# S5 of a two-layer hybrid trunk in steps of 4 tokens instead of 8, with its products in halves and quarters of the array

## The chip, the cores and the metric

The kernel runs on one core of a Trainium2 chip. Its time is the device time of one execution in microseconds (us); of several runs the median counts. A profile is one more execution, recorded by the hardware.

## The reference

Two residual layers, each with one input projection `h @ w_in` of the normed x (512 tokens, width 2048), four branches that share its columns (MLA attention, S5, RWKV-7, differential attention), a gate, and an output projection. The change touches S5 and the token shift of RWKV:

```python
for l in range(DEPTH):                                    # 2
    h = rms_norm(x, norm_g[l])
    proj = h @ w_in[l]
    c_q, c_kv, k_rope, u_s5, z_rwkv, q_d, k_d, v_d, gate = jnp.split(proj, points, axis=-1)
    ...
    x = x + (mixed @ w_out[l]).astype(x.dtype)

def s5_branch(u, ...):                                    # 32 groups of 16 channels, 64 complex states each
    bu = einsum('bsgc,gpc->bsgp', ug, bb)
    h  = associative_scan over s of h[s] = ab * h[s-1] + bu[s]
    y  = einsum('bsgp,gcp->bsgc', h_re, c_re) - einsum('bsgp,gcp->bsgc', h_im, c_im)
    ...                                                   # + d * u, gelu, gated linear unit

def rwkv7_branch(z, mu, ...):
    z = z + (z_prev - z) * mu                             # the lerp: z_prev is z one token before
```

## The kernel before

Matrices are held transposed, 128 channels on the partitions by 512 tokens. The projections make up most of the program: a column of 128 outputs is 16 steps of 128 inputs, and each step three products of 128x512, since float32 weights and inputs are split into a high and a low part (`XH`, `XL`, `wh`, `wl`). ScalarE casts `wh` (line 243), VectorE subtracts for `wl` (line 244); `big` keeps a ring of three such pieces. The products of a column add up in an accumulator `acc` (two in PSUM) or in one of the six banks `pb`, which everything else uses too.

The order of TensorE's work is written out as the program is built. A class `Clock` holds the planned time of TensorE, and the branches are generators, each of which says with `yield Y[...]` how many microseconds it needs before its next products can be ready; between them the columns of the projections are emitted. The orders of the other engines come from a scheduler with priorities: `tc.high_priority(offset=AHEAD)` moves work that frees an accumulator or prepares weights ahead, and `late` ties an instruction behind the latest weight piece.

In the input projection the columns are the low-rank one (`lo`), then r, k, v of the first and of the second pair of heads, then four of `u`, and so on. They are multiplied without the norm of x, and up to six of them wait (`pend`: two `acc`, four `pb`) until the norm's row `rx` is there. Then `evacuate` is called for each. For `lo` and r, k, v it calls `z_tile`: VectorE multiplies by the norm into `zr` (line 535), ScalarE makes `zd` = `zr` times (1 - mu) (line 537), and VectorE adds `zr` one token back times mu (line 538). `zr` and `zd` have one buffer each.

S5 takes 8 tokens as one step of its state, so that each group has 64 steps. `s5_tables` (line 367 on) makes, in layer 0 beside the first columns and in layer 1 during the output projection of layer 0, the powers of the transition (`pw`) and, in four blocks of 128x512, cosine and sine of each step's angle (`tq`, `tr`, `cs`, lines 469 to 479). Each of 8 units of a layer (`s5_unit`, 4 groups, two units at a time) has these products: transposes of AB into IN; K, from which DMAs lay out the triangular T; IN times U (inputs to states); and, after a rotation by the table, a scan over the steps and a rotation back into `H` (lines 913 to 930), T times U plus CA times H (line 126), which is the unit's output. GpSimd does the products with the sine, ScalarE the copies that swap real and imaginary halves (`sw`).

Of the kernel before, what the change touches and what calls it, by code (L numbers as in the profile page):

```python
# [64 lines left out]
for _n, _w in (("norm_g", 16), ("mu", 13), ("w0", 4), ("a0", 4), ("k_k", 4), ("k_a", 4),  # L65
# [8 lines left out]
PW = {"pr": (0, 9), "pi": (9, 18), "rr": (18, 26), "ri": (26, 34), "m8": (34, 35)}  # L74
NPW = 35
# [12 lines left out]
def consts():  # L88
# [13 lines left out]
    put("qidx", np.broadcast_to(np.arange(64), (128, 64)))  # L102
# [85 lines left out]
def trunk(ctx, tc, io, KT=16, depth=DEPTH):  # L188
# [41 lines left out]
    s5tab = dram("s5tab", [depth, 4, 128, 2, 512])  # L230
# [133 lines left out]
    def s5_tables(pl, l, pace):  # L364
# [34 lines left out]
        for n in (1, 2, 4):  # L399
# [7 lines left out]
        for i in range(8):  # L407
            A.copy(out=pw[:, :, PW["rr"][0] + i], in_=pr[:, :, 7 - i])
            A.activation(out=pw[:, :, PW["ri"][0] + i], in_=pi[:, :, 7 - i], func=AF.Copy, scale=C("sg"))
        m8 = pw[:, :, PW["m8"][0]]  # L410
        V.tensor_tensor(out=m8, in0=mag, in1=mag, op=ALU.mult)
        V.tensor_tensor(out=m8, in0=m8, in1=m8, op=ALU.mult)
        V.tensor_tensor(out=m8, in0=m8, in1=m8, op=ALU.mult)
# [21 lines left out]
        V.tensor_scalar(out=thi, in0=th, scalar1=8.0 / TWO_PI, scalar2=None, op0=ALU.mult)  # L435
# [6 lines left out]
        for q in range(4):  # L442
            g0 = 8 * q
            yield pace
# [32 lines left out]
            cs2 = pl.tile([128, 2, 8, 64], F32, name="cs2", tag="cs2", bufs=2)  # L477
# [52 lines left out]
    def z_tile(ps, mu, m1, rxr, out):  # L530
# [298 lines left out]

    def phases(d):  # L830

        return d.rearrange("(i c) (g q) -> (c g) i q", i=8, g=8)

    def s5_load(sp, l, e, uD):

# [7 lines left out]
        tab = sp.tile([128, 2, 4, 64], F32, name="tab", tag="tab", bufs=3)  # L843
# [531 lines left out]
    class Layer:  # L1375
# [185 lines left out]
        def in_proj(self, begun):  # L1561
            l, pend = self.l, []
            for i, (n, t) in enumerate(ORDER):
# [274 lines left out]
```

## Time and profile before

| | us |
|---|---|
| median of 3 runs | 1981.13 (1977.79 to 1984.48) |
| the profiled execution, its own time | 1977.86 |
| its span, first to last instruction | 1976.0 |
| TensorE busy | 1926.1 (97%) |
| VectorE busy | 1314.7 (67%) |
| ScalarE busy | 870.7 (44%) |
| GpSimd busy | 167.0 (8%) |

The granted clock of TensorE is 0.991 of full speed over the span; 1 is its level of 2.4 GHz, 0.5 that of 1.2 GHz. In the profile PE is TensorE's products, PEld its weight loads, DVE is VectorE, ACT ScalarE, POOL GpSimd. Products overlap one another, so what one costs is read from its start to the next start, not from its length. L126 is the line of the helper that records every product.

### The profile page before, as it was taken

What the parts mean: (1) busy time and instruction counts of PE and PEld (TensorE: products, weight loads), DVE (VectorE), ACT (ScalarE), POOL (GpSimd) and SP (SyncE); (2) the same over time, 40 slices, a digit from 0 to 9 for tenths busy, and PEclk for the clock granted to TensorE, in tenths of its full rate; (3) what the DMA queues carried; (4) which work ended last, traced back from release to release, by engine and by line L of the source; (5) the groups of instructions that cost most, each with busy time, mean ns of one, the idle gap of its engine ahead of it and who ended that gap; (6) DMA issues with size and microseconds to landing.
All of it is one profiled execution on the core that took longest, in us unless ns stands there. A gap on an engine that the chain in (4) does not pass through costs nothing.

```text
span 1976.0 us, 31426 instructions
## 1 busy us (share of the span) xinstructions
PE 1926.1 (97%) x10975; PEld 1565.9 (79%) x10975; DVE 1314.7 (67%) x2883; ACT 870.7 (44%) x1855; POOL 167.0 (8%) x222
## 2 busy tenths in 40 slices
PE   9979999999999999999999999999999999999997
PEld 7867887777778778888888788778788778788787
DVE  6887876556686578747855686674675667766453
ACT  6544335434235446534533334454332544554351
POOL 1101110022000010002001011101010000000001
PEclk9989999999999999999999999999999999999999
DMA  6453546455473437555743454365457326654553
GB/s 213 140 178 117 150 131 163 147 167 174 147 216 103 153 120 238 180 161 188 244 144 123 117 141 140 99 198 176 156 168 225 118 95 211 206 163 156 162 166 117
DMA packets 244734, 316.85 MB, mean 160 GB/s; under 512 B 83680, under 2 KB 109792, under 8 KB 244576
## 3 DMA queue, kind: packets, MB, share of 16 engines
q1 hardware_dynamic: 243200, 313.44, 51.4%
q8 instruction: 86, 1.41, 0.3%
q10 hardware_dynamic: 1376, 1.41, 0.2%
q14 instruction: 72, 0.59, 0.1%
HBM read 238.64 MB, written 73.76 MB: 158 GB/s over the span
## 4 chain that ended last, share of the span: by engine, by line
PE 48%; DMA 2%; DVE 1%; ACT 1%; issue 0%; POOL 0%; SPq 0%; DVEq 0%; ACTq 0%
PE acc L126 39%; PE pb L126 8%; PE pb L130 1%; DMA raw<-in_w_out_dram 1%; DMA yD<-do 0%; DMA xo<-xP 0%; DMA raw<-knD 0%; POOL smag L377 0%; DMA R<-qkD 0%; DVE wl L244 0%; DVE Fo L1647 0%; DMA zr<-yD 0%; ACT wh L243 0%; DMA y<-yD 0%; DVE xo L1613 0%
## 5 line engine op out<-in xcount | busy, mean ns | idle before, releaser
L126 PE MATMUL acc<-XH,wl 128*128 128x512 f32 x1600 | 653.3, 408 | 17.0 <-DVE zr L535 10.7
L126 PE MATMUL acc<-XL,wh 128*128 128x512 f32 x1600 | 627.5, 392 | 1.1 <-DVE XL L494 1.1
L126 PE MATMUL acc<-XH,wh 128*128 128x512 f32 x1600 | 628.1, 393 | 0.0
L243 ACT CAST wh<-raw 128x512 fp32r<-128x512 f32 x559 | 341.8, 617 | 549.0 <-PE acc L126 400.8
L244 DVE TENSOR_TENSOR wl<-raw,wh 128x512 fp32r<-128x512 f32 x559 | 385.8, 694 | 245.5 <-ACT wh L243 241.2
L126 PEld LDWEIGHTS acc<-XH,wl 128*128 128x128 f32 x1600 | 302.1, 189 | 91.8 <-DVE zr L535 11.2
L126 PEld LDWEIGHTS acc<-XH,wh 128*128 128x128 f32 x1600 | 301.7, 189 | 66.0
L126 PEld LDWEIGHTS acc<-XL,wh 128*128 128x128 f32 x1600 | 302.5, 189 | 58.3 <-DVE XL L494 2.7
L126 PE MATMUL acc<-MH,wl 128*128 128x512 f32 x448 | 177.8, 397 | 3.4 <-DVE xo L1613 2.6
L126 PE MATMUL acc<-MH,wh 128*128 128x512 f32 x448 | 174.9, 391 | 0.0
L126 PE MATMUL acc<-ML,wh 128*128 128x512 f32 x448 | 174.7, 390 | 0.0
L126 PEld LDWEIGHTS acc<-MH,wl 128*128 128x128 f32 x448 | 84.2, 188 | 21.9 <-DVE xo L1613 3.4
L126 PEld LDWEIGHTS acc<-MH,wh 128*128 128x128 f32 x448 | 84.1, 188 | 17.9
L126 PEld LDWEIGHTS acc<-ML,wh 128*128 128x128 f32 x448 | 84.2, 188 | 16.3
L1005 ACT ACTIVATE pt<-pb,nb,fc 128x128 f32<-128x128 f32 (+3 forms) x64 | 39.5, 617 | 30.3 <-DVE nb L1004 30.0
L1338 POOL TENSOR_TENSOR sr<-ss,cc 128x1 f32<-128x1 f32 x32 | 19.7, 615 | 326.7 <-DVE ss L1336 247.2
L689 DVE TENSOR_TENSOR tmp<-X 64x30 f32<-64x30 f32 (+14 forms) x120 | 39.7, 331 | 10.8 <-DMA X<-nD 8.4
L1003 DVE TENSOR_REDUCE mx<-pb 128x1 f32<-128x128 f32 (+3 forms) x96 | 45.9, 478 | 0.5
L801 POOL TENSOR_TENSOR rs<-vr,cc 128x16 f32<-128x16 f32 x4 | 12.1, 3028 | 383.1 <-DVE vr L799 383.1
L778 DVE SCALAR_TENSOR_TENSOR SV<-pb,ec,tmp 64x64 f32<-64x64 f32 x96 | 27.2, 283 | 23.6 <-PE pb L126 20.9
L693 DVE TENSOR_TENSOR X<-X,tmp 64x30 f32<-64x30 f32 (+14 forms) x120 | 39.2, 327 | 2.5
L1002 DVE TENSOR_TENSOR pb<-pb,cc 128x128 f32<-128x128 f32 x96 | 26.4, 295 | 21.5 <-PE pb L126 20.9
(408 smaller groups left out, 2804.3 us busy)
## 6 DMA issues: line engine op xcount, KB each, us to landing
raw<-in_w_in_dram SPq DMA_DIRECT2D x415, 256.0 KB, 3.5
raw<-in_w_out_dram SPq DMA_DIRECT2D x128, 256.0 KB, 3.5
gD<-stg SPq DMA_DIRECT2D x32, 256.0 KB, 3.4
xP<-stg SPq DMA_DIRECT2D x19, 256.0 KB, 2.1
xo<-xP SPq DMA_DIRECT2D x19, 256.0 KB, 3.6
zD<-stg SPq DMA_DIRECT2D x18, 256.0 KB, 3.0
s5tab<-cs SPq DMA_DIRECT2D x8, 512.0 KB, 4.7
tab<-s5tab SPq DMA_DIRECT2D x16, 256.0 KB, 4.5
```

The source lines that it names most:

```text
L126: return self.nc.tensor.matmul(out, lhsT=lhsT, rhs=rhs, **kw)
L130: return self.nc.tensor.transpose(out, in_, identity)
L243: x = A.copy(out=wh[:, :n], in_=raw[:, :n])
L244: y = V.tensor_sub(out=wl[:, :n], in0=raw[:, :n], in1=wh[:, :n])
L689: i = V.tensor_tensor(out=t2, in0=X[:, 0:j, j:j + 1].to_broadcast([64, j, n]), in1=X[:, j:j + 1, j + 1:32].to_broadcast([64, j, n]), op=AL ...
L693: V.tensor_tensor(out=X[:, 0:j, j + 1:32], in0=X[:, 0:j, j + 1:32], in1=t2, op=ALU.add)
L778: V.scalar_tensor_tensor(out=SVs[s][T, c + 1, h], in0=po[h][T, 64:128], scalar=ec[T, h, c:c + 1], in1=T1[T, h], op0=ALU.mult, op1=ALU.add)
L801: G.tensor_tensor(out=rs, in0=vr, in1=C("mhalf", 0, 16), op=ALU.pow)
L1002: V.tensor_tensor(out=ps[:, qb * 128:n], in0=ps[:, qb * 128:n], in1=C("neg"), op=ALU.add)
L1003: V.tensor_reduce(out=mx, in_=ps[:, 0:n], axis=AX.X, op=ALU.max)
L1005: A.activation(out=pt, in_=ps[:, 0:n], func=AF.Exp, scale=fcol[:, qb:qb + 1], bias=nb, accum_out=sm)
L1338: G.tensor_tensor(out=sr, in0=ss, in1=C("mhalf", 0, 1), op=ALU.pow)
```

## The change

S5's step becomes 4 tokens. The power tables shrink (9 and 8 powers to 5 and 4), CA from 576 to 320 and AB from 512 to 256 elements a partition; the steps of a group become 128, so the tables for the angles double (8 blocks of 128x512 per layer instead of 4), and so do v, sw, gs and H. A step's inputs of one group now fill 64 partitions, so two groups share the array: IN times U runs in 64-row halves, T times U in 64x64 quarters, CA times H in 64-column halves, 128 columns each, into two banks. One scan over the four groups becomes four scans, since each now takes its factor as a broadcast. The table is loaded at a unit's start, no longer one unit ahead. The planner's entries s1 and s3 and the pace of the tables change. In `z_tile`, `zd` is made by VectorE for the first nine columns of a layer (seven of them are z tiles).

```diff
-PW = {"pr": (0, 9), "pi": (9, 18), "rr": (18, 26), "ri": (26, 34), "m8": (34, 35)}
-NPW = 35
+PW = {"pr": (0, 5), "pi": (5, 10), "rr": (10, 14), "ri": (14, 18), "m4": (18, 19)}
...
-    "z12": 1.5, "ch": 1.4, "h3": 2.58, "h1": 2.73, "h2": 2.54, "gn": 16.96, "s1": 11.34, "s2": 2.8,
-    "s3": 13.65, "glu": 35.7, "lr": 18.14, "kvr": 6.4, "uv": 2.21, "mr": 27.22, "mh": 9.45, "mu": 5.78,
+    "z12": 1.5, "ch": 1.4, "h3": 2.58, "h1": 2.73, "h2": 2.54, "gn": 16.96, "s1": 10.0, "s2": 2.8,
+    "s3": 15.0, "glu": 35.7, "lr": 18.14, "kvr": 6.4, "uv": 2.21, "mr": 27.22, "mh": 9.45, "mu": 5.78,
...
+        for e in range(8):
+            g0 = 4 * e
             yield pace
-
-            qb = C("qidx").unsqueeze(1).to_broadcast([128, 8, 64])
-            tq = pl.tile([128, 8, 64], F32, name="tq", tag="tq", bufs=2)
-            tr = pl.tile([128, 8, 64], F32, name="tr", tag="tr", bufs=2)
-            hb = thi[:, g0:g0 + 8].unsqueeze(2).to_broadcast([128, 8, 64])
-            lb = tlo[:, g0:g0 + 8].unsqueeze(2).to_broadcast([128, 8, 64])
+            if e % 2 == 0:
+                inputs(e // 2)
+                yield pace
+
+            qb = C("qidx").unsqueeze(1).to_broadcast([128, 4, 128])
...
-            cs2 = pl.tile([128, 2, 8, 64], F32, name="cs2", tag="cs2", bufs=2)
+            cs2 = pl.tile([128, 2, 4, 128], F32, name="cs2", tag="cs2", bufs=2)
             sincos(tq, cs2[:, 1], cs2[:, 0], scale=6.2831850)
...
-    def z_tile(ps, mu, m1, rxr, out):
+    def z_tile(ps, mu, m1, rxr, out, quick):
...
         with tc.high_priority(offset=AHEAD):
             V.tensor_tensor(out=zr[:, 1:], in0=ps, in1=rxr, op=ALU.mult)
             d = zp.tile([128, S], F32, name="zd", tag="zd", bufs=1)
-            A.activation(out=d, in_=zr[:, 1:], func=AF.Copy, scale=m1)
+            if quick:
+                V.tensor_scalar(out=d, in0=zr[:, 1:], scalar1=m1, scalar2=None, op0=ALU.mult)
+            else:
+                A.activation(out=d, in_=zr[:, 1:], func=AF.Copy, scale=m1)
             V.scalar_tensor_tensor(out=out, in0=zr[:, 0:S], scalar=mu, in1=d, op0=ALU.mult, op1=ALU.add)
...
-        tab = sp.tile([128, 2, 4, 64], F32, name="tab", tag="tab", bufs=3)
-        SP.dma_start(out=tab.rearrange("p a g q -> p a (g q)"), in_=s5tab[l, t, :, :, 256 * hf:256 * hf + 256])
...
+        pw, bb, U = loaded.pop(e)
+        tab = sp.tile([128, 2, 4, 128], F32, name="tab", tag="tab", bufs=2)
+        SP.dma_start(out=tab.rearrange("p a g q -> p a (g q)"), in_=s5tab[l, e])
...
-        CA, W = t3("CA", 9), t3("W", 9)
+        CA, W = t3("CA", 5), t3("W", 5)
...
-        late(V.tensor_tensor(out=CA, in0=bj(pr), in1=bc(c1, 9), op=ALU.mult))
-        V.tensor_tensor(out=W, in0=bj(pi), in1=bc(c2, 9), op=ALU.mult)
+        late(V.tensor_tensor(out=CA, in0=bj(pr), in1=bc(c1, 5), op=ALU.mult))
...
         yield Y["s1"]
         ps = pb()
-        for g in range(4):
-            PE.transpose(ps[:, g * 128:(g + 1) * 128], AB[:, g].rearrange("p i c -> p (i c)"), ident)
-        A.copy(out=IN.rearrange("p g x -> p (g x)"), in_=ps)
...
+        for p in range(2):
+            PE.transpose(ps[:, p * 128:p * 128 + 128], AB[:, 2 * p:2 * p + 2].rearrange("p h i c -> p (h i c)"), ident)
+        A.copy(out=IN.rearrange("p a x -> p (a x)"), in_=ps[:, 0:256])
...
         for g in range(4):
-            PE.matmul(ps[32 * g:32 * g + 16, 0:128], lhsT=b1[:, g],
-                      rhs=CA[:, g, 0:8].rearrange("p j c -> p (j c)"), start=True, stop=True)
+            PE.matmul(ps[32 * g:32 * g + 16, 0:64], lhsT=b1[:, g],
+                      rhs=CA[:, g, 0:4].rearrange("p j c -> p (j c)"), start=True, stop=True)
...
-        psI = pb()
-        for g in range(4):
-            PE.matmul(psI[:, 64 * g:64 * g + 64], lhsT=IN[:, g], rhs=U8[:, g], start=True, stop=True)
...
-        A.copy(out=swf[0:64], in_=psI[64:128, 0:256])
-        A.copy(out=swf[64:128], in_=psI[0:64, 0:256])
...
+        psI = pb(), pb()
+        for p in range(2):
+            for h, x in enumerate(HS):
+                PE.matmul(psI[h][:, 128 * p:128 * p + 128], lhsT=IN[x, p], rhs=U[x, p], start=True, stop=True)
+        sw, v = t2("sw"), t2("v")
+        for h in range(2):
+            y = psI[h][:, 0:256].rearrange("p (a q) -> p a q", q=128)
+            for a, b in (HS, HS[::-1]):
+                A.copy(out=half(sw, h)[a], in_=y[b])
+            V.tensor_tensor(out=half(v, h), in0=y, in1=half(tab[:, 0], h), op=ALU.mult)
         G.tensor_tensor(out=sw, in0=sw, in1=tab[:, 1], op=ALU.mult)
         V.tensor_tensor(out=v, in0=v, in1=sw, op=ALU.add)
...
-        gs = t2("gs")
-        V.tensor_tensor_scan(out=gs.rearrange("p g q -> p (g q)"), data0=m8.rearrange("p g q -> p (g q)"),
-                             data1=v.rearrange("p g q -> p (g q)"), initial=0.0, op0=ALU.mult, op1=ALU.add)
+        gs = t2("gs", 1)
+        for g in range(4):
+            V.tensor_tensor_scan(out=gs[:, g], data0=m4[:, g].to_broadcast([128, 128]), data1=v[:, g], initial=0.0,
+                                 op0=ALU.mult, op1=ALU.add)
...
         yield Y["s3"]
-        psY = pb()
-        for g in range(4):
-            PE.matmul(psY[:, 64 * g:64 * g + 64], lhsT=T[:, g], rhs=U8[:, g], start=True, stop=False)
-            PE.matmul(psY[:, 64 * g:64 * g + 64], lhsT=CA[:, g, 1:9].rearrange("p j c -> p (j c)"),
-                      rhs=H[:, g, 0:64], start=False, stop=True)
...
+        psY = pb(), pb()
+        for h, x in enumerate(HS):
+            for p, y in enumerate(HS):
+                PE.matmul(psY[h][y, 0:128], lhsT=T[x, p], rhs=U[x, p], start=True, stop=False)
+        for h in range(2):
+            for p, y in enumerate(HS):
+                g = 2 * p + h
+                PE.matmul(psY[h][y, 0:128], lhsT=CA[:, g, 1:5].rearrange("p j c -> p (j c)"), rhs=H[:, g, 0:128],
+                          start=False, stop=True)
...
     def tables(l):
         with sub("tab", l) as st:
-            yield from s5_tables(st, l, 2.5 if l == 0 else 3.0)
+            yield from s5_tables(st, l, 1.6 if l == 0 else 1.8)
...
                 if l in rx:
                     for x in pend:
-                        self.evacuate(*x)
+                        self.evacuate(*x, i < 9)
```

The program's order on TensorE for the output of the first two units of layer 0 (`acc` is a projection's accumulator, numbers tell buffers apart). Before, the first unit's run, with T and CA in turn four times (the first of the pairs shown):

```order
L126 MATMUL acc_2013<-XH_78,wh_2064 128x512
L126 MATMUL pb_2071<-U8_1596,T_1830 128x64
L126 MATMUL pb_2071<-H_1909,CA_1685 128x64
L126 MATMUL pb_2071<-U8_1596,T_1830 128x64
L126 MATMUL pb_2071<-H_1909,CA_1685 128x64
```

After, the run of both units:

```order
L126 MATMUL acc_2097<-XH_78,wh_2118 128x512
L126 MATMUL pb_2125<-U_1643,T_1863 64x128 x2
L126 MATMUL pb_2126<-U_1643,T_1863 64x128 x2
L126 MATMUL pb_2125<-H_1956,CA_1734 64x128 x2
L126 MATMUL pb_2126<-H_1956,CA_1734 64x128 x2
L126 MATMUL pb_2140<-U_1651,T_1887 64x128 x2
L126 MATMUL pb_2141<-U_1651,T_1887 64x128 x2
L126 MATMUL pb_2140<-H_1986,CA_1755 64x128 x2
L126 MATMUL pb_2141<-H_1986,CA_1755 64x128 x2
L126 MATMUL acc_2097<-XH_78,wl_2119 128x512
```

Each product is now 64x128 in place of 128x64, all of T stand ahead of those of CA, and the second unit stands right behind the first, where before nine products of a column lay between them.

VectorE's order around the sixth and seventh `zr` of layer 0 (`tq`, `tr`, `cs` are S5's tables, `stg` the lerp's output, `tmp` RWKV's). Before:

```order
L476 TENSOR_TENSOR tq<-tq,tr 128x512 x2
L583 SCALAR_TENSOR_TENSOR tmp<-cc,tmp 128x512
L244 TENSOR_TENSOR wl<-raw,wh 128x512
L535 TENSOR_TENSOR zr<-pb,rxr 128x512
L479 TENSOR_SCALAR cs_1017<-cs_1017,cc 128x512
L479 TENSOR_SCALAR cs_1153<-cs_1153,cc 128x512
L335 TENSOR_SCALAR cs_1017<-cs_1017 128x512
L592 TENSOR_SCALAR tmp<-tmp 128x512
L335 TENSOR_SCALAR cs_1153<-cs_1153 128x512
L538 SCALAR_TENSOR_TENSOR stg<-zr,pvt,zd 128x512
L535 TENSOR_TENSOR zr<-acc,rxr 128x512
L538 SCALAR_TENSOR_TENSOR stg<-zr,pvt,zd 128x512
```

After:

```order
L541 TENSOR_TENSOR zr<-pb,rxr 128x512
L476 TENSOR_TENSOR tq<-tq,tr 128x512
L478 TENSOR_TENSOR tr<-cc,stlo 128x512
L544 TENSOR_SCALAR zd<-zr,dv 128x512
L478 TENSOR_TENSOR tr<-cc,stlo 128x512
L479 TENSOR_TENSOR tq<-tq,tr 128x512
L547 SCALAR_TENSOR_TENSOR stg<-zr,pvt,zd 128x512
L479 TENSOR_TENSOR tq<-tq,tr 128x512
L480 TENSOR_SCALAR tr<-tq 128x512
L541 TENSOR_TENSOR zr<-acc,rxr 128x512
L480 TENSOR_SCALAR tr<-tq 128x512
L481 TENSOR_TENSOR tq<-tq,tr 128x512
```

Between these two `zr` stood two more steps of a table block (lines 479 and 335) and RWKV's row; now there stand the lerp's `zd` and six instructions of the next table block.

VectorE's order around the second unit's `H`. Before:

```order
L915 TENSOR_TENSOR v<-v,sw 128x256
L535 TENSOR_TENSOR zr<-acc,rxr 128x512
L883 TENSOR_TENSOR W<-pw,bb 128x4x128
L244 TENSOR_TENSOR wl<-raw,wh 128x512
L920 SCALAR_TENSOR_TENSOR gs<-m_1941,v 128x256
L538 SCALAR_TENSOR_TENSOR stg<-zr,pvt,zd 128x512
L927 TENSOR_TENSOR v<-gs,tab 128x256
L917 COPY m_2347<-pw 128x256
L918 MEMSET m_2347 128x4
L244 TENSOR_TENSOR wl<-raw,wh 128x512
L930 TENSOR_TENSOR H<-v,sw 128x4x64
```

After:

```order
L937 SCALAR_TENSOR_TENSOR gs<-pw,v 128x128 x3
L547 SCALAR_TENSOR_TENSOR stg<-zr,pvt,zd 128x512
L937 SCALAR_TENSOR_TENSOR gs<-pw,v 128x128
L244 TENSOR_TENSOR wl<-raw,wh 128x512
L898 TENSOR_TENSOR AB<-pw,bb 128x256
L944 TENSOR_TENSOR v<-gs,tab 128x512
L893 TENSOR_TENSOR CA<-pw,bb 128x320
L898 TENSOR_TENSOR AB<-pw,bb 128x256
L900 TENSOR_TENSOR AB<-AB,W 128x256
L895 TENSOR_TENSOR CA<-CA,W 128x320
L698 TENSOR_TENSOR tmp<-X 64x30
L947 TENSOR_TENSOR H<-v,sw 128x4x128
```

Between the scan and `H` stood one `wl` and the start of another unit's chain (L917, L918); now the scan is four instructions, and CA and AB of the next units, one `wl` and a row of RWKV (L698) stand there.

## Rows read from the trace of the kernel before

**Rows 1.** Busy time of TensorE: us, share of the span, instructions.

```profile
PE 1926.1 (97%) x10975; PEld 1565.9 (79%) x10975; DVE 1314.7 (67%) x2883; ACT 870.7 (44%) x1855; POOL 167.0 (8%) x222
```

**Rows 2.** TensorE's waits by releaser: us in total, times, longest.

```profile
PE acc L126 <- DVE zr L535: 10.7, 1, 10.7
PE acc L126 <- DVE wl L244: 5.5, 7, 1.8
...
PE pb L126 <- DVE H L930: 2.1, 1, 2.1
```

**Rows 3.** TensorE's timeline: start us, us, operation, stationary tile, xcount.

```profile
186.04 0.60 PE L130 MATMUL pb<-cc,AB 128*128 128x128 f32 x4
186.56 0.41 PE L126 MATMUL pb<-CA,bb 128*16 128x128 f32 x8
186.91 0.66 PE L130 MATMUL pb<-cc,AB 128*128 128x128 f32 x4
...
188.48 1.10 PE L126 MATMUL pb<-U,IN 128*128 128x64 f32 x8
189.39 0.48 PE L126 MATMUL acc<-XH,wl 128*128 128x512 f32 x1
...
203.42 0.33 PE L126 MATMUL pb<-U,T 128*128 128x64 f32 x2
...
205.12 0.48 PE L126 MATMUL acc<-XH,wl 128*128 128x512 f32 x1
```

**Rows 4.** TensorE's timeline at products in parts of the array.

```profile
195.20 1.16 PE L126 MATMUL pb<-Q,SV 64*128 64x128 f32 x16
196.29 0.50 PE L126 MATMUL acc<-XH,wl 128*128 128x512 f32 x1
...
300.55 0.45 PE L126 MATMUL pb<-SV,NM 64*64 64x64 f32 x8
300.93 0.45 PE L126 MATMUL pb<-SV,BKt 128*64 128x64 f32 x8
...
304.39 0.39 PE L126 MATMUL acc<-XL,wh 128*128 128x512 f32 x1
304.61 0.39 PE L126 MATMUL acc<-XH,wh 128*128 128x512 f32 x1
304.93 0.69 PE L126 MATMUL pb<-SV,Q 128*64 128x64 f32 x16
305.55 0.50 PE L126 MATMUL acc<-XH,wl 128*128 128x512 f32 x1
```

**Rows 5.** VectorE's timeline before the seventh `zr`.

```profile
87.24 0.69 DVE L469 TENSOR_TENSOR tq<-cc,sthi 128x512 f32<-128x512 f32 x1
87.84 0.68 DVE L244 TENSOR_TENSOR wl<-raw,wh 128x512 fp32r<-128x512 f32 x1
88.45 0.42 DVE L470 TENSOR_SCALAR tr<-tq 128x512 f32<-128x512 f32 x1
88.78 0.76 DVE L335 TENSOR_SCALAR cs<-cs 128x512 f32<-128x512 f32 x2
...
106.73 0.98 DVE L335 TENSOR_SCALAR cs<-cs 128x512 f32<-128x512 f32 x1 [1.74 <-ACT cs L334]
...
110.06 0.69 DVE L535 TENSOR_TENSOR zr<-acc,rxr 128x512 f32<-128x512 f32 x1
```

**Rows 6.** Windows: us, busy PE, PEld, DVE, ACT, POOL (count), clock, DMA, GB/s.

```profile
72.80:110.10 37.30, 27.28 (x119) 21.43 (x117) 34.40 (x67) 27.52 (x44) 3.15 (x8) 0.92 0.46 153
110.10:209.70 99.60, 95.00 (x514) 76.29 (x514) 78.25 (x133) 39.96 (x74) 11.66 (x22) 0.96 0.51 148
908.30:1001.00 92.70, 91.87 (x405) 75.50 (x404) 79.15 (x183) 48.41 (x91) 0.30 (x5) 1.00 0.67 216
```

**Rows 7.** The window behind TensorE's wait for `zr`, same columns.

```profile
110.81:120.00 9.19, 9.19 (x35) 8.04 (x36) 6.40 (x12) 3.47 (x5) 1.96 (x2) 0.63 0.52 144
```

**Rows 8.** VectorE's timeline, first unit of S5.

```profile
200.39 0.41 DVE L930 TENSOR_TENSOR H<-v,sw 128x256 f32<-128x256 f32 x1
```

More of the change, by code (lines that the diff above doesn't have):

```diff
@@ L55 @@
 for _n, _w in (("ident", 128), ("bones", 128), ("maskS", 128), ("neg", 128), ("reset", 512),
-               ("qidx", 64), ("bo2", 2), ("one", 2), ("invm", 1), ("invd", 1), ("ssin", 1),
+               ("qidx", 128), ("bo2", 2), ("one", 2), ("invm", 1), ("invd", 1), ("ssin", 1),
                ("sg", 1), ("mhalf", 32), ("e", 32)):
@@ L101, in consts @@
     put("reset", np.broadcast_to((np.arange(512) % 64 != 0), (128, 512)))
-    put("qidx", np.broadcast_to(np.arange(64), (128, 64)))
+    put("qidx", np.broadcast_to(np.arange(128), (128, 128)))
     put("bo2", (p[:, None] // 64 == np.arange(2)[None, :]))
@@ L398, in s5_tables @@
         V.tensor_tensor(out=pi[:, :, 1], in0=mag, in1=sn, op=ALU.mult)
-        for n in (1, 2, 4):
+        for n in (1, 2):
             br = pr[:, :, n:n + 1].to_broadcast([128, 32, n])
@@ L406, in s5_tables @@
         V.tensor_scalar(out=pw[:, :, a:b], in0=pr, scalar1=C("sg"), scalar2=-1.0, op0=ALU.mult, op1=ALU.mult)
[L407 to L413, printed above, removed]
+        for i in range(4):
+            A.copy(out=pw[:, :, PW["rr"][0] + i], in_=pr[:, :, 3 - i])
+            A.activation(out=pw[:, :, PW["ri"][0] + i], in_=pi[:, :, 3 - i], func=AF.Copy, scale=C("sg"))
+        m4 = pw[:, :, PW["m4"][0]]
+        V.tensor_tensor(out=m4, in0=mag, in1=mag, op=ALU.mult)
+        V.tensor_tensor(out=m4, in0=m4, in1=m4, op=ALU.mult)
         SP.dma_start(out=s5pw[l], in_=pw)
@@ L441, in s5_tables, with inputs @@
         cs = []
-        for q in range(4):
+        def inputs(q):
             g0 = 8 * q
-            yield pace
             sb = pl.tile([128, 2, 2, 64], F32, name="ssb", tag="ssb", bufs=2)
@@ L482, in s5_tables @@
             yield pace
-            if q:
-                late(SP.dma_start(out=s5tab[l, q - 1], in_=cs[q - 1].rearrange("p a g q -> p a (g q)")))
+            if e:
+                late(SP.dma_start(out=s5tab[l, e - 1], in_=cs[e - 1].rearrange("p a g q -> p a (g q)")))
         yield pace + 4.0
-        late(SP.dma_start(out=s5tab[l, 3], in_=cs[3].rearrange("p a g q -> p a (g q)")))
+        late(SP.dma_start(out=s5tab[l, 7], in_=cs[7].rearrange("p a g q -> p a (g q)")))
     def absorb(sp, k, x, pvt, sqs, first):
@@ L883, in s5_unit @@
-        V.tensor_tensor(out=W[:, :, 0:8], in0=bj(ri), in1=bc(b2, 8), op=ALU.mult)
-        V.tensor_tensor(out=AB, in0=AB, in1=W[:, :, 0:8], op=ALU.add)
-        IN = sp.tile([128, 4, 128], F32, name="IN", tag="IN", bufs=1)
+        AB, W = t3("AB", 4), t3("W", 5)
+        V.tensor_tensor(out=AB, in0=bj(rr), in1=bc(b1, 4), op=ALU.mult)
+        V.tensor_tensor(out=W[:, :, 0:4], in0=bj(ri), in1=bc(b2, 4), op=ALU.mult)
+        V.tensor_tensor(out=AB, in0=AB, in1=W[:, :, 0:4], op=ALU.add)
+        IN = sp.tile([128, 2, 128], F32, name="IN", tag="IN", bufs=2)
@@ L899, in s5_unit @@
-        T = sp.tile([128, 4, 128], F32, name="T", tag="AB", bufs=2)
+            A.copy(out=K[:, g], in_=ps[32 * g:32 * g + 16, 0:64])
+        T = sp.tile([128, 2, 64], F32, name="T", tag="AB", bufs=2)
         G.memset(T, 0.0)
-        for i in range(8):
-            SP.dma_start(out=T[16 * i:16 * i + 16, :, 16 * i:128], in_=K[:, :, 0:128 - 16 * i])
+        for h in range(2):
+            for i in range(4):
+                o = 64 * h + 16 * i
+                SP.dma_start(out=T[o:o + 16, :, 16 * i:64], in_=half(K, h)[:, :, 0:64 - 16 * i])
@@ L951, in load @@
             for x, d in ((u, uD), (y, ysD)):
-                SP.dma_start(out=x.rearrange("p (i q) -> p i q", i=8), in_=phases(d[t]))
+                SP.dma_start(out=x.rearrange("p (i q) -> p i q", i=4), in_=phases(d[t]))
             return u, y
@@ L1378, in __init__ @@
             self.yD = dram(f"yD{l}", [16, 128, S])
-            for n, shape in (("uD", [4, 128, S]), ("ysD", [4, 128, S]), ("qkD", [1024, S]),
+            for n, shape in (("uD", [4, 64, 2 * S]), ("ysD", [4, 64, 2 * S]), ("qkD", [1024, S]),
                              ("vD", [4, 128, S]), ("aD", [7, 128, S]), ("knD", [4, 128, S]),
@@ L1472, in others, with evacuate @@
             self.finish("others")
[L1475 removed]
+        def evacuate(self, n, t, ps, quick):
             l, rxr = self.l, rx[self.l][1]
```

78 lines of the change are left out of this document (40 added, 38 removed).

## The prediction

> **What bounds the kernel now.** I read the table of busy time first. TensorE is busy for 97% of the span [rows 1], so a microsecond that TensorE no longer works is a microsecond off the end, unless a wait takes its place. The list of TensorE's waits by what ended them comes next [rows 2]: one wait of 10.7 us for VectorE's `zr`, seven for `wl` with 5.5 us together, one of 2.1 us for `H`. The change touches the causes of all three. So two questions stand: what S5's products cost TensorE before and after, and whether VectorE, which gets more to do, comes later at those three places.
>
> **S5's products on TensorE.** There are 8 units in each of 2 layers, 16 in all. From start to start in TensorE's timeline [rows 3] one unit costs 0.52 (four transposes, 186.04 to 186.56), 0.35 (K, to 186.91), 0.91 (IN times U, 188.48 to 189.39) and 1.70 (T times U and CA times H in turn, 203.42 to 205.12): 3.48 us, 55.7 us in all. A record of the full-array products thus takes 0.91/8 = 0.114 or 1.70/16 = 0.106 us.
>
> The trace has products in parts of the array, in RWKV [rows 4]. A 64-row half (128 columns moved, the new form of IN times U) takes 1.09/16 = 0.068 us a record, a 64-column half with 64 columns moved 0.62/16 = 0.039, quarters 0.38/8 = 0.048. So parts of the array do run side by side: a record in a half that moves 128 columns takes less than a full-array record that moves 64. After the change I take: two transposes 0.29 (half of 0.52 and a start), K with half the columns 0.25 (between 0.18 and 0.35), IN times U 8 x 0.068 and a start = 0.61, T times U 0.38 (quarters, by the row), CA times H 8 x 0.068 and a start = 0.57. Together 2.10, which saves 1.38 a unit: **-22.1 us**. The ends: all 34 records at 0.039 cost 1.33, which saves 34.4; a price of 0.106 to 0.114 for each record, as for the full array, makes 0.91 + 0.85 + 0.85 + 0.26 + 0.35 = 3.22 and saves only 4.2. I stay near the tiled rows, since they are the same shapes.
>
> A tiled run has an entry and an exit. Before the run at 304.93 the step is 0.32 (from 304.61) where a plain one is 0.22 (from 304.39), and the first product behind it lasts 0.50 where plain ones last 0.39 [rows 4]: 0.10 + 0.11, about 0.2 us. Each unit has one more such run in effect, since the runs of two units stand together: 16 x 0.2 = **+3.2 us** (ends 0 and 9.6, three runs a unit).
>
> The Trainium skill, page "TensorEngine Tiling (Array Packing)", section "Key Properties" of "Tiling Modes", says that a change of tiling mode drains the array, and its page "TensorE: Matmul & The Clock Gate" puts a drain at about 175 ns. By those figures, as an estimate, four changes a unit would cost 16 x 4 x 0.175 = 11.2 us in place of 3.2, and the sum would come out 8 us higher, at -0.6. The rows show 0.1 us at a change, so the measured step decides here.
>
> **VectorE before the seventh `zr`.** Until the norm of x is ready, TensorE runs ahead; six columns then wait to be evacuated, and TensorE stands until 110.8, when the seventh `zr` (start 110.06) has freed its accumulator [rows 2, 5]. In this stretch VectorE is busy 34.40 of 37.30 us [rows 6], so what is put in front of that `zr` delays it. VectorE's prices, start to start [rows 5]: 0.60 for two operands of 128x512 (87.24 to 87.84), 0.33 for one operand (88.45 to 88.78). By the program's order 62 instructions stand from the first to the seventh `zr` before and 80 after, at those prices 32.6 and 39.6 us: 7.0 more, six of them lerp products at 0.33, the rest table work. Against it, the lerp no longer waits for ScalarE, and VectorE's idle time in this stretch is 37.30 - 34.40 = 2.90; I credit 2.7 of it (1.74 alone is before the row at 106.73, and that one is a sine that stays on ScalarE). The `zr` comes 7.0 - 2.7 = **+4.3 us** later (ends: +7.0 with nothing credited, and -10.7 if the stall closes, below). The first `zr` starts as before: the rows ahead of it sum to 47.4 and 46.9 us.
>
> **VectorE up to the second unit of S5.** From the first `zr` to the second unit's `H` the order holds 197 instructions before (104.8 us) and 246 after (124.4): 19.6 us more, of which 7.0 are counted above. The other 12.6 us lie between 110.1 and 209.7, where VectorE is free for 99.60 - 78.25 = 21.35 us [rows 6]. That is cover, but not all in the right place: after the seventh `zr` a block of table rows now stands ahead of the next `wl`, and the second `H` is already 2.1 us late [rows 2]. Ends 0 and 12.6; I take **+3 us**, near the hidden end.
>
> **Tables of layer 1.** The same four more blocks of tables fall on the seam of the layers, 91.2 us of work in place of 75.7: 15.5 more. From 908.3 to 1001.0 VectorE has 92.70 - 79.15 = 13.55 us free [rows 6], so **+2 us** are left over (ends 0, since more room follows, and 15.5).
>
> **S5's chain on the vector engines.** Per unit the halves of `sw` are now four copies, GpSimd's two products double in size and one scan becomes four. I estimate 2.5 to 3.5 us more per unit, while the planner's entry s3 gives 1.35 more. The first unit's `H` ends at 200.80 [rows 8], 2.6 us ahead of the unit's run at 203.42 [rows 3]; so a unit like it has cover for the difference. Where it is gone, at the pair's second unit, the wait grows: **+1 us** (ends 0, and 8 with four such units). U's and ys's longer DMA runs, the shorter power tables and the smaller CA and AB lie beside all this and count as nothing; CA and AB save VectorE some 0.7 us a unit, which is in the counts above for the first pair.
>
> **Sum.** -22.1 + 3.2 + 4.3 + 3 + 2 + 1 = -8.6 us. The profiled execution took 1977.86 us, so 1969.3; the median of the runs, 1981.13, lies 3.3 above it, so about 1972 us for the runs.
>
> **Rivals.**
> *B, the stall closes.* The two waits of the lerp on ScalarE are what kept VectorE from the seventh `zr`, and with them gone the 10.7 us go, with the half-speed stretch behind them: from 110.81 to 120.00 the granted clock is 0.63 [rows 7], so TensorE loses 9.19 x 0.37 = 3.4 us. Then -14.1 stands in place of +4.3: 1954 us. For it speaks that `zr` and `zd` have one buffer each, so that each lerp holds up the next evacuation; against it, that VectorE was 92% busy in this stretch and gets more.
> *C, the other side: VectorE's table work falls on TensorE.* All 19.6 us of layer 0 reach TensorE, as a longer stall at the seventh `zr` and late `wl` and `H` behind it, with a second restart at half speed (3.4): -22.1 + 3.2 + 19.6 + 3.4 + 2 + 1 = +7.1, 1988 us. It decides once layer 0 loses more than 22.1 - 3.2 - 3 = 15.9 us. For it: VectorE is the last to end at all three places. Against it: the 21.35 us free.
> *D, the parts of the array don't run side by side* in these shapes: the saving is 4.2 and the sum +9.3, 1990 us. Against it stand the tiled rows; for it, that T and CA now write one bank in turns from different halves.
> *E, the changes of shape cost more*: at three runs a unit with 0.2 us each, 9.6 in place of 3.2, the sum is -2.2 and the time 1979 us. For it: T times U and CA times H have shapes of their own, so the array changes more often than before. Against it: no row shows more than 0.1 us at one change.
> The Trainium skill's rule on drains, cited above, would end beside E, at about 1981 us.
>
> **Chances.** Forecast 0.48, B 0.20, C 0.18, D 0.04, E 0.05, and 0.05 for something that I don't see. About 0.3% (6 us) is what a measurement of this kernel can tell from no change: under 1975 is faster, over 1987 slower. The forecast's own range is 1963 to 1982, so a third of it is "same"; B is faster; two thirds of C, D and some of the unseen are slower, and E is "same": faster 0.52, same 0.27, slower 0.21. The range of 1950 to 1989 leaves out the better part of B's lower half and of C's and D's upper.
>
> **What would show it.** In the new trace: S5's runs at about 2.1 us a unit, the runs of tiled products with steps like [rows 4] (if IN times U takes 0.9 us or more, D is right); the wait for `zr` in the list, at about 15 us (B: gone or a few us; C: 20 and more); waits for `wl` and `H` of some 5 and 3 us; no TensorE wait near the seam of the layers above 2 us. I am wrong if the waits of [rows 2] change by more than 10 us in sum, or S5's runs by less than 0.8 or more than 1.8 us a unit.

## Result and the profile after

The changed kernel takes 2010.73 us in the median of 4 runs (2005.79 to 2011.19), the kernel before 1980.2. The ratio is 1.0149 (1.0131 to 1.0166): 30 us slower, where 8.6 us faster was forecast and 1989 was the upper end. By the prediction's own sign of being wrong, the waits of [rows 2] for `zr`, `wl` and `H` went from 18.3 to 41.2 us, by more than its 10 us, while S5's runs cost 1.4 us less a unit, inside its limits of 0.8 and 1.8.

The list of TensorE's waits of the changed kernel (us in total, times, longest), which answers to [rows 2], and below it the busy times of the page, which answer to [rows 1]:

```profile
PE acc L126 <- DVE zr L541: 16.4, 1, 16.4
PE pb L126 <- DVE H L947: 15.1, 4, 7.4
PE acc L126 <- DVE wl L244: 9.7, 12, 3.1
PE acc L126 <- ACT XH L498: 6.3, 2, 6.0
```

```profile
PE 1925.8 (96%) x10943; PEld 1550.2 (77%) x10943; DVE 1358.7 (68%) x2988; ACT 881.0 (44%) x1899; POOL 185.4 (9%) x222
```

TensorE is as busy as before (1926.1), although its work became less: a stretch at half clock counts as busy. I add up both timelines of TensorE, from each product's start to the next start (up to the last product), and set apart the waits and, as an estimate, what half clock adds (half of each such stretch, outside waits). S5's products go from 56.4 to 33.9 us, all others from 1859.3 to 1863.8, waits from 38.2 to 71.8, and half clock from 10.2 to 27.9: -22.5 + 4.5 + 33.6 + 17.7 = 33.3, the difference of the spans (2009.3 and 1976.0). So S5's saving is there, and waits with the clock behind them cost 51 us. Up to the last product the kernel before has four stretches at half clock, 27 us long together, the changed kernel nine, 75 us long.

TensorE's timeline of the changed kernel at the first pair of units, which answers to [rows 3] (start us, us, operation, stationary tile, count):

```profile
196.50 0.38 PE L130 MATMUL pb<-cc,AB 128*128 128x128 f32 x2
196.81 0.31 PE L126 MATMUL pb<-CA,bb 128*16 128x64 f32 x8
...
199.80 1.11 PE L126 MATMUL pb<-U,IN 64*128 64x128 f32 x16
200.74 1.59 PE L126 MATMUL pb<-Q,SV 64*128 64x128 f32 x16
...
215.52 0.45 PE L126 MATMUL pb<-U,T 64*64 64x128 f32 x8
215.90 0.66 PE L126 MATMUL pb<-H,CA 128*64 128x128 f32 x8
216.49 0.45 PE L126 MATMUL pb<-U,T 64*64 64x128 f32 x8
224.34 1.12 PE L126 MATMUL pb<-H,CA 128*64 128x128 f32 x8 [7.40 <-DVE H L947]
```

IN times U of both units is one run of 16 records, 0.94 us or 0.059 a record; T times U takes 0.38 (215.52 to 215.90), CA times H 0.59. These are near the prices that the prediction took from [rows 4] (0.068 a record, 0.38 and 0.57). But the second unit's output waits 7.4 us for `H`. What happens in its chain, in the timelines of GpSimd and of VectorE:

```profile
202.69 1.30 POOL L933 TENSOR_TENSOR sw<-sw,tab 128x512 f32<-128x512 f32 x1 [4.93 <-ACT sw L931]
209.55 1.29 POOL L942 TENSOR_TENSOR sw<-sw,tab 128x512 f32<-128x512 f32 x1 [5.56 <-ACT sw L941]
211.09 1.29 POOL L933 TENSOR_TENSOR sw<-sw,tab 128x512 f32<-128x512 f32 x1 [0.25 <-ACT sw L931]
...
219.72 2.71 POOL L942 TENSOR_TENSOR sw<-sw,tab 128x512 f32<-128x512 f32 x1 [1.48 <-ACT sw L941]
```

```profile
223.49 0.20 DVE L698 TENSOR_TENSOR tmp<-X 64x30 f32<-64x30 f32 x1 [2.18 <-DMA X<-nD]
223.61 0.67 DVE L947 TENSOR_TENSOR H<-v,sw 128x512 f32<-128x512 f32 x1
```

GpSimd does the sine products of the first unit at 202.69 and 209.55, and those of the second after them, at 211.09 and 219.72, here in 2.71 us. VectorE then stands for 2.18 us at an RWKV row that waits for a DMA, with `H` behind it; 1.1 us of this lie behind the end of GpSimd's product at 222.43, before which `H` could not start. From its IN times U to its `H` (224.28) the second unit needs 24.5 us; the plan gives it 15.0. Before, its IN times U came 2.9 us after the first's (191.36 and 188.48) and its `H` 18.3 us after that:

```profile
191.36 1.10 PE L126 MATMUL pb<-U,IN 128*128 128x64 f32 x8
209.27 0.41 DVE L930 TENSOR_TENSOR H<-v,sw 128x256 f32<-128x256 f32 x1
```

The seam of the layers, VectorE and then TensorE of the changed kernel:

```profile
1021.25 0.68 DVE L481 TENSOR_TENSOR tq<-tq,tr 128x512 f32<-128x512 f32 x1
1021.85 0.48 DVE L484 TENSOR_SCALAR cs<-cs,cc 128x512 f32<-128x512 f32 x1
1022.24 0.68 DVE L1620 TENSOR_TENSOR xo<-acc,xo 128x512 f32<-128x512 f32 x1
```

```profile
1023.77 0.80 PE L126 MATMUL acc<-XH,wl 128*128 128x512 f32 x1 [5.96 <-ACT XH L498]
```

The tables of layer 1 still run (1021.25, 1021.85) where the last `xo` of the output projection is due, and TensorE waits 5.96 us for the `XH` made from it. Of the 4.40 us that VectorE works from 1017.84 to this `xo`, three table rows take 1.3. Before, the last table row came at 966, 30 us ahead of the seam, and the first product of layer 1 did not wait for the last `xo` at all, but stood ahead of it:

```profile
997.26 0.39 PE L126 MATMUL acc<-XH,wl 128*128 128x512 f32 x1
998.02 0.69 DVE L1596 TENSOR_TENSOR xo<-acc,xo 128x512 f32<-128x512 f32 x1 [0.41 <-issue]
```

This is a matter of order. The output projection's order of columns is built from those that were done ahead (`part` in `out_proj`). With 9 done ahead, as before, column 0 comes first; with 10, as in the changed kernel, it comes last; and the first product of a layer reads the `XH` of column 0.

The windows behind the three longest waits (us, busy times with counts, clock, DMA, GB/s), the first of which answers to [rows 7]:

```profile
116.70:124.00 7.30, 7.27 (x25) 6.46 (x26) 7.30 (x16) 4.39 (x8) 2.27 (x2) 0.50 0.28 99
224.30:232.00 7.70, 7.66 (x31) 6.07 (x32) 6.66 (x22) 1.35 (x4) 0.11 (x1) 0.75 0.50 143
1023.70:1031.00 7.30, 7.22 (x18) 5.34 (x19) 2.80 (x6) 1.68 (x4) 0.14 (x2) 0.55 0.74 242
```

### The profile page after: what moved, and what is told of

Read it like the earlier page. It is cut to its first block, busy times and chain, and to the rows that moved or that the text cites. A ratio compares the mean times of both kernels' runs of the same rounds, so it can differ in the third digit from the quotient of the medians.

```text
span 2009.3 us, 31589 instructions
## 1 busy us (share of the span) xinstructions
PE 1925.8 (96%) x10943; PEld 1550.2 (77%) x10943; DVE 1358.7 (68%) x2988; ACT 881.0 (44%) x1899; POOL 185.4 (9%) x222
## 4 chain that ended last, share of the span: by engine, by line
PE 56%; DVE 7%; DMA 6%; issue 3%; ACT 2%; SPq 1%; POOL 1%; DVEq 0%; ACTq 0%; POOLq 0%
PE acc L126 44%; PE pb L126 11%; PE pb L130 2%; DVE wl L244 1%; DMA xo<-xP 1%; DMA raw<-in_w_out_dram 1%; DMA qs<-qrD 1%; DMA gt<-ysD 0%; ACT wh L243 0%; DVE tmp L698 0%; DMA w2a<-gD 0%; POOL sdt L377 0%; POOL smag L377 0%; DVE X L702 0%; DMA ks<-aD 0%
## 5 line engine op out<-in xcount | busy, mean ns | idle before, releaser
L126 PE MATMUL acc<-XH,wl 128*128 128x512 f32 x1600 | 656.7, 410 | 32.2 <-DVE zr L541 16.4
L698 DVE TENSOR_TENSOR tmp<-X 64x30 f32<-64x30 f32 (+14 forms) x120 | 41.0, 342 | 11.2 <-DMA X<-nD 8.6
L126 PE MATMUL acc<-MH,XL 128*128 128x256 f32 x128 | 36.6, 286 | 1.0 <-DVE xo L1637 1.0
```

Source lines behind the costliest of these rows:

```text
L126: return self.nc.tensor.matmul(out, lhsT=lhsT, rhs=rhs, **kw)
L698: i = V.tensor_tensor(out=t2, in0=X[:, 0:j, j:j + 1].to_broadcast([64, j, n]), in1=X[:, j:j + 1, j + 1:32].to_broadcast([64, j, n]), op=AL ...
```

## Experiments

Numbers in brackets are ratios to the kernel before with their 95% intervals; the changed kernel is at 1.0149. The kernel before was timed beside each group of runs (medians of 1976.5 to 1980.2 us), so differences between runs are taken from the ratios; with these intervals they are good to some 3 to 5 us. A "step" counts TensorE's products of the projections, 6336 in each kernel: the time of the same step in two traces tells how far one is behind.

**Half the tables** (`a_halftab`). Every second block of table arithmetic is left out, ScalarE's sines with it.

```diff
         for e in range(8):
...
+            if e % 2 == 0:
                 V.tensor_tensor(out=tq, in0=qb, in1=hb, op=ALU.mult)
...
```

> The changed kernel with the arithmetic of every second block of S5's angle tables left out (its place is filled with the block before, so the output is not that of S5); all else stays. Theory W, VectorE's doubled table work makes the longer wait for zr and the wait at the seam of the layers: the wait for zr falls from 16.4 to 8 to 11 us, the wait of 6.0 us for XH near 1024 us goes with the half-speed stretch behind it, and the time falls by 18 to 25 us, to 1986 to 1993. Rival R1, the table work is hidden and the loss is all in S5's units: within 4 us of 2010.7.

1995.87 us, 1.0097 (1.0080 to 1.0115): 10 us back, about half of what was expected. The wait for `zr` is again that of before, the waits for `H` stay, and the seam keeps a wait of 4 us, although the last table row now comes at 979, 37 us ahead of the product that waits (1015.99):

```profile
PE pb L126 <- DVE H L949: 15.4, 4, 7.7
PE acc L126 <- DVE zr L543: 10.9, 1, 10.9
...
PE acc L126 <- ACT XH L500: 4.4, 2, 4.0
```

**More time for each unit** (`a_s3`): `"s3": 15.0` becomes 24.0.

> The changed kernel with one number of the planner raised: s3, the time that a unit of S5 is given from its IN times U to its output, 24.0 in place of 15.0. Theory W, two units now start together and share VectorE, ScalarE and GpSimd, so the second is due too early: the waits for H fall from 15.1 to under 3 us, three or four half-speed stretches go with them, and the time falls by 12 to 22 us, to 1989 to 1999. Rival R2, the chain is bound elsewhere (the longer S5 puts the wait at another product, or is given back where MLA begins later): within 5 us of 2010.7.

2006.36 us, 1.0140 (1.0122 to 1.0159): within what R2 said. No wait for `H` is left in the list, and at step 2448, near the end of layer 0's input projection, this kernel is 12.6 us ahead of the one before where the changed kernel is 17.5 behind. From there to step 3312 it loses 30.5 us again: S5 ends 36 us later in the plan, with it the branches, and less of the output projection is left beside which the tables could run.

**The lerp** (`a_lerp_act`, `b_lerp`): `self.evacuate(*x, i < 9)` with `False` for the condition; and the diff's hunk of `z_tile` alone on the kernel before.

> The changed kernel with the lerp product back on ScalarE in all columns. Theory W, the lerp on VectorE costs about 0.33 us a column in the stretch before the seventh zr and saves waits of the same size: the wait for zr stays within 3 us of 16.4, the time within 4 us of 2010.7. Rival R3, the lerp on VectorE is what lengthened the stall: 6 us less wait and about 8 us less time. Rival B of the prediction, in weaker form (the lerp on VectorE helps, and the tables hide it): 5 us or more longer.

> The kernel before with the lerp product of the first nine columns on VectorE, nothing else changed. Theory W: the wait for zr stays within 3 us of 10.7, the time within 4 us of 1980. Rival R3: the wait is 13 us or more and the time 1984 or more. Rival B of the prediction: the wait falls below 4 us, and the time to about 1966 to 1972.

2010.02 us, 1.0159 (1.0146 to 1.0173), and 1979.31 us, 1.0010 (1.0001 to 1.0020). The lerp costs or gives nothing that can be told. It does lengthen the wait for `zr`, from 10.8 to 16.4 with the doubled tables and from 10.7 to 13.0 without them, against theory W's 3 us in the first; but between steps 432 and 576 the kernel without it loses 5.9 us against the one before, the changed kernel 3.2, and by step 1152 they stand 19.0 and 21.8 us behind. So most of the shorter wait is lost again at later ones.

**Tables elsewhere** (`a_mid`, `a_mid_s3`, `a_pool`, `a_pace`): tables of layer 1 in `others` of layer 0 behind GLU, alone and with s3 at 24; every second block's arithmetic on GpSimd; the paces of before.

```diff
-            PE.spawn(tables(l + 1), 1)
...
                 yield from s5_glu(gp, l, P, self.uD, self.ysD, self.yout)
+            if l + 1 < depth:
+                yield from tables(l + 1)
```

```diff
+            X = G if e % 2 else V
...
-            V.tensor_tensor(out=tq, in0=qb, in1=hb, op=ALU.mult)
+            X.tensor_tensor(out=tq, in0=qb, in1=hb, op=ALU.mult)
```

> The changed kernel with the tables of layer 1 made in layer 0, between GLU and MLA, where VectorE is half free, and no longer beside the output projection; all else stays. Theory W, the table work on the seam is what makes TensorE wait there: the wait of 6.0 us for XH near 1024 us and the half-speed stretch behind it go, the ten microseconds lost from step 3168 to step 3312 of the projections fall to 2 or less, and the time falls by 8 to 14 us, to 1997 to 2003. Rival R5, the tables only move: MLA and the differential attention come later by as much, and the time stays within 5 us of 2010.7.

> Both edits at once: tables of layer 1 between GLU and MLA, and s3 at 24.0. With s3 alone the projections of layer 0 ran 13 us ahead of the kernel before and lost 30 us on the seam. Theory W, that loss is the tables, squeezed into an output projection with less left to do: without them the gain stays, and the time is 1960 to 1980, at or below the kernel before. Rival R6, the loss is the later end of the branches themselves: 1995 or more.

> The changed kernel with the multiplications, roundings and differences of every second block of S5's tables on GpSimd in place of VectorE; the same results. Theory W, VectorE's load is the cause at zr and at the seam: the wait for zr falls to 9 to 13 us, the loss on the seam to under 7, and the time to 1993 to 2002, near that with half the blocks left out (1996). Rival R7, GpSimd's products are slow beside a busy VectorE (its products of 128x512 took 1.3 to 3.3 us in the units) and the tables come later than S5 wants them: 2008 or more.

> The changed kernel with the planner's steps between the parts of a table block at 2.5 and 3.0 us as before the change, in place of 1.6 and 1.8. Theory W, it is the sum of VectorE's work that is too much, not its order: the wait for zr falls to 11 to 14 us, but what is saved comes back as waits for wl and H or as a later S5, and the time stays within 6 us of 2010.7, with the seam worse by up to 6 us. Rival R8, the faster pace put the table rows ahead of the evacuations and is the cause: 2002 or less.

2051.19 us, 1.0369 (1.0348 to 1.0389); 2057.52, 1.0407 (1.0388 to 1.0427); 2029.04, 1.0267 (1.0248 to 1.0285); 2008.81, 1.0160 (1.0142 to 1.0177). In `a_mid` the step from 3168 to 3312 costs 1.9 us in place of 10.0, as expected, but this doesn't show the tables' share alone: with 12 columns done ahead in place of 10, column 0 is no longer last. The branches end later, with 25 us lost between steps 2880 and 3024: W's total failed in both runs, and a later branch is a bound of its own. `a_pool` is slower, as R7 said, but not because S5 gets its tables late: the waits for `H` stay at 15.0 us and that for `zr` falls to 10.6, as W said, but those for `wl` rise from 9.7 to 28.7. VectorE's groups of `a_pool` between 937 and 1020 us (count, busy us, mean ns, idle before):

```profile
L244 DVE TENSOR_TENSOR wl<-raw,wh 128x512 fp32r<-128x512 f32 x23 | 23.1, 1002 | 0.8 <-ACT wh L243 0.7
...
L508 DVE TENSOR_TENSOR sqs<-sqs,sq 128x512 f32<-128x512 f32 x10 | 9.6, 964 | 0.0
L1621 DVE TENSOR_TENSOR xo<-acc,xo 128x512 f32<-128x512 f32 x11 | 7.5, 685 | 2.0 <-DMA xo<-xP 1.6 <-PE acc L126 0.3
```

`wl` takes 1002 ns on average where it takes 686 in the changed kernel, `xo`, which reads PSUM, still 685. The paces change nothing in sum (and leave the wait for `zr` at 16.4, where W had 11 to 14).

**The units apart** (`a_stag`, `a_swdve`, `a_stag_sw`, `a_stag_half`): the second unit's first wait in the plan is 8 us longer; both sine products on VectorE; both; and the first with half the tables.

```diff
             loaded[e] = s5_load(sp, l, e, uD)
-            yield Y["ld"]
+            yield Y["ld"] + 8.0 * e
```

```diff
-        G.tensor_tensor(out=sw, in0=sw, in1=tab[:, 1], op=ALU.mult)
+        V.tensor_tensor(out=sw, in0=sw, in1=tab[:, 1], op=ALU.mult)
...
-        G.tensor_tensor(out=sw2, in0=sw2, in1=tab[:, 1], op=ALU.mult)
+        V.tensor_tensor(out=sw2, in0=sw2, in1=tab[:, 1], op=ALU.mult)
```

> The changed kernel with the second unit of S5 of each layer begun 8 us later in the plan, so that two units run in turn and not together; s3 stays at 15.0. Theory W, a pair that starts together is what makes H late: the waits for H fall from 15.1 to under 4 us, three half-speed stretches go, S5 ends 8 us later and not 36 as with s3 at 24, and the time falls by 8 to 16 us, to 1995 to 2003. Rival R6, a later S5 gives back what the waits save: within 5 us of 2010.7.

> The changed kernel with the two products of each unit by the sine table on VectorE in place of GpSimd. Theory W, GpSimd's products of 128x512 (1.3 to 3.3 us, and VectorE slower beside them) make the chain of a unit long: at 0.6 us each the waits for H fall to 8 to 11 us and the time by 4 to 9 us. Rival R9, VectorE is what is short: 32 products more (19 us) make waits for wl and H longer, and the time rises by 3 us or more.

> Both edits at once: the second unit 8 us later and the sine products on VectorE. Theory W: no wait for H above 1 us is left, and the time is 1989 to 1999. Rival R9 with R6: 2008 or more.

> The second unit 8 us later, and the arithmetic of every second table block left out (so the output is not that of S5). Theory W, the two causes are apart and add up: 10 to 14 us for the tables as before and 8 to 16 for the pairs, so 1978 to 1992; what then stands above the kernel before is the seam, where half the tables already left 7 us. Rival R10, they do not add up, because one wait covers for the other: within 4 us of 1996.

1986.09 us, 1.0042 (1.0027 to 1.0057); 2014.67, 1.0187 (1.0171 to 1.0204); 1988.23, 1.0053 (1.0038 to 1.0067); 1971.45, 0.9971 (0.9958 to 0.9984). Eight microseconds in the plan give back 21, more than the 8 to 16 expected. The waits of `a_stag` hold no `H` at all; the first are:

```profile
PE acc L126 <- DVE zr L541: 16.4, 1, 16.4
PE acc L126 <- DVE wl L244: 10.9, 11, 3.1
PE pb L126 <- ACT PT L1039: 6.9, 9, 1.4
PE acc L126 <- ACT XH L498: 3.9, 1, 3.9
```

Half clock costs 14.2 us here in place of 27.9, the waits 56.7 in place of 71.8. The sine products on VectorE make the waits for `H` longer (23.9 us, 6 times), those for `wl` not (9.6); the time rises as R9 said. With the units apart they change nothing that can be told (1.0053 and 1.0042). With half the tables as well another 14 us go: the two causes add up, and 1971 is below the 1978 to 1992 expected.

**Which layer's tables, and whose gain** (`a_stag_half0`, `a_stag_half1`, `a_stag_act`, `b_stag`): half the tables in one layer alone; two instructions of each block on ScalarE; the units apart in the kernel before.

```diff
-            sincos(tq, cs2[:, 1], cs2[:, 0], scale=6.2831850)
-            V.tensor_scalar(out=cs2[:, 1], in0=cs2[:, 1], scalar1=C("sg"), scalar2=-1.0,
-                            op0=ALU.mult, op1=ALU.mult)
+            sincos(tq, cs2[:, 1], cs2[:, 0], scale=-6.2831850, act=True)
+            A.activation(out=cs2[:, 1], in_=cs2[:, 1], func=AF.Copy, scale=C("sg"))
```

> Second unit 8 us later, and every second table block's arithmetic left out in layer 0 alone (so the output is not that of S5). Both layers' blocks left out gave 1971.5 against 1986.1 with all blocks. Theory W, most of these 14.6 us is layer 0's: the wait for zr from 16.4 to 10.9, its half-speed stretch from 20.5 to 13.7 us long, and the wait for wl near 168 us with its stretch; 9 to 11 us, so 1975 to 1977, and the seam stays as it is (the step from 3168 to 3312 at 8 to 9 us). Rival R11, most of it is the seam's: 1981 to 1984.

> Second unit 8 us later, and every second table block's arithmetic left out in layer 1 alone (so the output is not that of S5). Theory W: layer 0 stays at 16.4 us for zr, the seam's step falls from 8.8 to about 4, and the time is 1981 to 1983. Rival R11: 1975 to 1978.

> Second unit 8 us later, and two of the ten instructions of each table block moved from VectorE to ScalarE (the sign of the sine and 1 - 2 s^2 of the cosine); the results are the same. It takes 0.73 us of VectorE's work a block away, 5.8 us a layer, a third of what the four more blocks of a layer cost. Theory W: a third of the 14.6 us comes back, the wait for zr falls to 12 to 15 us, and the time is 1979 to 1984. Rival R12, ScalarE is as full as VectorE in these stretches and casts wh later: 1986 or more.

> The kernel before with the second unit of S5 begun 8 us later, nothing else changed. Theory W, before the change the two units were apart by 2.9 us and their chains shorter, with one wait for H of 2.1 us: the wait and its half-speed stretch of 6.8 us go at most, and the time stays within 6 us of 1977 (the gain of 21 us from the same edit on the changed kernel repairs a loss that the change made). Rival R13, the later second unit is a gain of its own, from another order of the branches: 1965 or less.

1977.17 us, 0.9998 (0.9986 to 1.0009); 1982.33, 1.0022 (1.0010 to 1.0033); 1981.34, 1.0013 (1.0001 to 1.0025); 1971.13, 0.9967 (0.9955 to 0.9980). Against `a_stag` half of layer 0's tables are worth 0.44% (8.7 us), half of layer 1's 0.20% (4 us, hardly clear of the intervals). The seam keeps 4.2 us (steps 3168 to 3312) with half of layer 1's tables. The units apart are a gain of 6.5 us in the kernel before too, so that, if the gains add, about 15 of the 21 us repair what the change lost.

**Two last versions** (`a_stag14_act`, `a_stag_act_pace`): `a_stag_act` with 14.0 in place of 8.0, and with layer 0's pace at 2.5.

> The version with two table instructions on ScalarE, and the second unit 14 us later in place of 8, half of a unit's 27.8 us in the plan, so that the units alternate evenly. Theory W, at 8 us no wait for H is left, so the pairs' cause is gone and more distance only delays S5 by 6 us: within 5 us of 1981. Rival R14, units of even distance load VectorE and the clock more evenly (fewer half-speed stretches in 250 to 310 us): 1968 to 1976, below the kernel before.

> The same version with the second unit 8 us later and the pace of layer 0's tables at 2.5 us as before the change, layer 1's left at 1.8. With both old paces the projections were 7 us less behind at the end of layer 0 than with the new ones, and lost this on the seam. Theory W, VectorE's load at the start of layer 0 is the larger part of the tables' cost, so spreading it gives 3 to 8 us: 1973 to 1978. Rival R8 reversed, S5 begins 20 us later and the branches end later: 1984 or more.

1982.51 us, 1.0018 (1.0007 to 1.0029), and 1984.16, 1.0026 (1.0017 to 1.0035): the distance of 8 us was enough, and the slower pace gives nothing (the time is at R8's bound). No complete version of the change gets below the kernel before; the kernel before with its units apart does.

## Why the prediction was wrong

- **S5's products**: right. -22.1 was forecast, -22.5 came. The other products grew by 4.5 us against 3.2 for the entries and exits; but they grew by about 4 us in `b_stag` too, whose products are those of before, so the entries have no clean price here. The Trainium skill's drains ("TensorEngine Tiling (Array Packing)", "Key Properties"), 11.2 us as estimated, are more than all of that (the estimate took about 175 ns from "TensorE: Matmul & The Clock Gate", section "Single matmul latency", and left out the page's further term for the columns moved); the measured sum decides.
- **S5's chain, "+1 us (ends 0, and 8)"**: this step failed. The waits for `H` went from 2.1 to 15.1 us, and with the clock behind them the pairs cost about 15 us (21 with what the kernel before would gain too), beyond the upper end of 8. I compared the longer chain of one unit with the cover of the first unit, 2.6 us. The order showed that both units' runs now stand together, and I took from it only the price of an entry. The second chain runs behind the first on engines that both share, so its time was the one to compare with s3: 24.5 us against 15.0.
- **Half clock**: the sum has no term for it. The longest waits (`zr`, `XH`, the four for `H`, one for `wl`) each had a stretch at half clock behind them, many short ones had none; together the stretches cost 17.7 us more than before. Only rivals B and C had such a price, 3.4 us.
- **VectorE in layer 0, +4.3 and +3**: the size was near. The wait for `zr` grew by 5.7 us, and half the tables give back 8.7 in all. But the 2.7 us credited to the lerp did not come: the lerp on VectorE lengthens this wait, by 2.3 us in `b_lerp` and by 5.6 against `a_lerp_act`.
- **The seam, +2**: too small. Steps 3168 to 3312 lost 10.0 us (8.8 in `a_stag`, of which half the tables of layer 1 give back 4.6). I read 13.55 us of free time in [rows 6] as one stock. But the tables began later against the seam (GpSimd's first table row at 916.40 us after, 894.00 before, with the projections 17 us later), and one more column had been done ahead (20 `xP` in the page, 19 before), so that less of the output projection lay beside them. That column also put column 0 last in the order, which no term of the prediction has: in `a_halftab`, with as many table rows as before and none of them near the seam, the same steps still lose 6.9 us. How the 10.0 us divide between order and tables no run shows by itself.
- **Rivals**: B is refuted by the lerp's runs. C gave the right side with another price: VectorE's tables alone cost 13 to 14 us and would not have turned 18 us of saving. D is refuted by the tiled rows, E by the other products' growth of 4.5 us in all against its 9.6.

Together: -18.0 us on TensorE's products, about +15 for the pairs and +13 to 14 for the tables make some +10; the other 20 stay open. They show when both causes are undone: `a_stag_half` (0.9971) is no faster than `b_stag` (0.9967), although its products cost TensorE 18 us less; its waits are 43.7 against 34.1 us and its half clock 12.3 against 4.1. Split at step 3312, one column behind the seam, almost all of this lies in layer 0: waits of 32.1 against 24.4 us and half clock of 12.2 against 3.9, in four stretches that `b_stag` doesn't have (at 252, 279, 490 and 999 us). Behind the seam the waits are 11.2 against 9.5, half clock is the same, and of the 9.9 us that S5's products save there 7.3 reach the end. The waits in layer 0 are spread over many small groups (`wl`, RWKV, MLA, the seam), and no run took them away. That the cheaper S5 brings each branch's work to VectorE closer together would fit, but wasn't tried.

## What to carry to other kernels

When a step of a planned pipeline becomes cheaper, look at what now stands next to what: two chains that start together share every engine behind them, and the due time is that of the second one. Price a new wait of the bounding engine together with the half-clock stretch that may stand behind it. And free time of a helper engine counts only where it lies ahead of the due time, not as a sum over a window. Where a program builds an order from counts, look at what a count of one more puts last.

## What was not expected of the hardware

VectorE's instructions on SBUF were longer while GpSimd worked on tables beside them: of the 23 `wl` of `a_pool` shown above, the 15 that overlapped a GpSimd instruction took 1.17 us on average (up to 1.78), the 8 others 0.69. Those that read PSUM were not: the 5 of 11 `xo` that overlapped one took 0.69 us like the others. And the length of a half-clock stretch didn't follow the wait ahead of it: 3.4 us long at the wait of 2.29 us that ends at 261.58, 10.2 us at one of 0.74 us that ends at 296.73, among products in parts of the array:

```profile
261.00:269.00 8.00, 7.42 (x31) 5.95 (x32) 7.41 (x20) 1.24 (x4) 0.10 (x1) 0.79 0.75 219
296.00:304.00 8.00, 7.27 (x79) 6.29 (x80) 6.37 (x15) 2.10 (x6) 0.11 (x1) 0.52 0.64 191
```
